# Hybrid block: intermediate stores on GpSimd's DMA queue, and two normed blocks turned from SBUF

## The chip, the cores and the metric

The kernel runs on one core of one Trainium2 chip. The metric is the device time of one execution, in microseconds (us). Engines are called as the profile calls them: PE (TensorE matmul), PEld (its weight load), DVE (VectorE), ACT (ScalarE), POOL (GpSimd) and SP (SyncE). SP computes nothing here; its queue issues most of the DMAs. A DMA issued by POOL stands in POOL's own instruction stream: POOL works its rows off in order, and a row that waits holds everything behind it. The same holds for SP.

## The reference

Two equal layers work on 1024 rows of 1024 fp32 numbers. Each is a mixer (four different heads, not touched here) and a feed-forward part, and both are wrapped in norms. What matters for this change is the end of the second layer:

```python
x = x + rms_norm(y @ w_out, g_post_mix)
h = rms_norm(x, g_pre_ffn)
x = x + rms_norm(conv_ffn(h, ...), g_post_ffn)

def conv_ffn(h, w_up, conv_w, conv_b, w_down):
    a, b = jnp.split(h @ w_up, 2, axis=-1)
    a = causal_dwconv(a, conv_w) + conv_b          # three taps along the rows
    return (jax.nn.gelu(a, approximate=True) * b) @ w_down
```

`w_up` has 2 x 2816 columns, that is 22 blocks `f` of 128 for `a` and as many for `b`.

## The kernel before, in words

All products are of fp32 accuracy: every operand is split into a high part (an ACT cast) and a low part (a DVE subtraction), and three matmuls give one product. The rows are worked in two halves of 512 (`h` 0 and 1), a half in four blocks `b` of 128.

**The last layer's feed-forward part** runs in these stages, in this order:

1. For half 0 the first six `f` are made early and plainly, in the midst of the mixer of half 1: `plain_up` (L1038) computes `c`, the gated result of one `f`, and stores it to a DRAM buffer `gD`.
2. `out(l, 1, y, True)` (L976) makes `y @ w_out` for the four blocks of half 1, and `norms` (L310) makes the two norms of each block. The normed blocks stand in four SBUF tiles, `oqf`, `okt`, `org` and `osu` (blocks 0 to 3). L324 also stores each to a DRAM buffer `hnD`; the blocks of half 0 were stored there earlier in the same way.
3. `plain_down` (L1048) multiplies the six early `f` of half 0 with `w_down` and stores the sums (`accD`).
4. `up_phase` takes new pools over the same SBUF, `rows` (L1088) names seven pairs of tiles (`A11`, `S1`, `S2`, `A12`, `S3`, `Q4`, `A22`, high and low), and `build` (L1095) fills them for one half. What follows is a fast matrix product of the Strassen-Winograd kind: seven products in place of eight, on sums of row blocks and column halves. `build` works on pairs of blocks. For each pair it loads two normed blocks from `hnD` (tiles `hn`), makes four sums on POOL (tiles `sa` and `sb`), turns the seven operands by 28 transposes on PE into seven PSUM banks, and puts each bank into its tile by an ACT cast (L1120) and a DVE subtraction (L1121). In the text that follows, one such cast with its subtraction is a "put".
5. `up_f` (L1133) makes one `f`: it loads the weight rows (`wraw`), makes seven weight operands `w` from them (ACT casts L1145, DVE subtractions L1146 and DVE sums L1150), runs the seven products (L1129 to L1131), and the gate (L1197 to L1202: ACT, two DVE, ACT with the gelu, two DVE), and stores `c` to `gD` (L1203). It runs first for `f` 0 and 1 of half 1 alone, right after `build(l, 1)`. Then comes `build(l, 0)`, and then all others: `f` 2 to 5 for half 1 alternate with `f` 6 to 21 for both halves.
6. `down_full` (L1205) loads `gD` and `w_down` again (tiles `graw` and `wraw`), splits both into tiles `g`, and adds all up; `end_block` makes the last norm.

**What sets the order.** A scheduler puts each engine's instructions into one fixed row when the program is built, by priorities in the code (`high_priority`) and by when tiles come free; on the chip each engine and each queue works its row off in order and waits by semaphores. Pools over the same SBUF are another source of waits: a tile of `up_phase` can only be written when the tile of the mixer that lay there has been read for the last time.

## Time and profile before

| what | us |
|---|---|
| median of 3 timed runs | 2526.83 (2521.61 to 2527.08) |
| profiled execution, its own time | 2522.4 |
| its span in the trace | 2520.6 |
| mean granted PE clock in it | 0.981 |
| PE busy | 2423.0 (96%) |
| DVE busy | 1777.1 (71%) |
| ACT busy | 971.6 (39%) |
| POOL busy | 251.7 (10%) |
| DMA, all queues | 281.33 MB, mean 112 GB/s |

Of the DMA bytes 266.37 MB go by the hardware queue that SP feeds and 12.65 MB by POOL's. In the trace a row has a start, a length, the engine, the source line, what it writes and reads, how many instructions it joins (x2), and, in brackets, the idle time of the engine ahead of it with what ended it. A row of SPq is the issue of a DMA, not the transfer.

### The profile page before, as it was taken

What the parts mean: (1) busy time and instruction counts of PE and PEld (TensorE: products, weight loads), DVE (VectorE), ACT (ScalarE), POOL (GpSimd) and SP (SyncE); (2) the same over time, 40 slices, a digit from 0 to 9 for tenths busy, and PEclk for the clock granted to TensorE, in tenths of its full rate; (3) what the DMA queues carried; (4) which work ended last, traced back from release to release, by engine and by line L of the source; (5) the groups of instructions that cost most, each with busy time, mean ns of one, the idle gap of its engine ahead of it and who ended that gap; (6) DMA issues with size and microseconds to landing.
All of it is one profiled execution on the core that took longest, in us unless ns stands there. A gap on an engine that the chain in (4) does not pass through costs nothing.

```text
span 2520.6 us, 36318 instructions
## 1 busy us (share of the span) xinstructions
PE 2423.0 (96%) x14020; PEld 2023.0 (80%) x14020; DVE 1777.1 (71%) x3659; ACT 971.6 (39%) x1510; POOL 251.7 (10%) x351
## 2 busy tenths in 40 slices
PE   8989998999999999899999999989888999998998
PEld 7968887877788987787778898877767888886887
DVE  8895699765655888955565589886567876664547
ACT  6333452423333453342332255233345444434212
POOL 2321103000000022200000001211003000000000
PEclk9999999999999999999999999999898999998999
DMA  5233343322233552222222355323363222215424
GB/s 185 72 90 111 126 135 92 103 80 76 80 100 109 161 166 84 76 94 77 84 84 85 124 167 188 92 82 110 117 226 118 101 92 83 77 59 201 141 67 151
DMA packets 100496, 281.33 MB, mean 112 GB/s; under 512 B 30482, under 2 KB 30802, under 8 KB 99812
## 3 DMA queue, kind: packets, MB, share of 16 engines
q1 hardware_dynamic: 96548, 266.37, 32.2%
q0 software_dynamic: 3776, 12.65, 1.5%
q8 instruction: 110, 1.80, 0.3%
q14 instruction: 62, 0.51, 0.1%
HBM read 239.11 MB, written 39.88 MB: 111 GB/s over the span
## 4 chain that ended last, share of the span: by engine, by line
PE 77%; DVE 14%; DMA 3%; issue 3%; ACT 2%; POOL 0%; SPq 0%; DVEq 0%; ACTq 0%; POOLq 0%
PE psg L213 9%; PE psg L214 9%; PE psg L212 9%; PE psg L1286 3%; PE psg L1288 3%; PE psg L1287 3%; DVE pr L839 3%; PE psg L233 3%; PE psg L1129 3%; PE psg L1131 3%; PE psg L1130 3%; PE psg L234 3%; PE psg L235 3%; DVE wlo L203 2%; DVE A L841 2%
## 5 line engine op out<-in xcount | busy, mean ns | idle before, releaser
L212 PE MATMUL psg<-hT,whi 128*128 128x512 f32 x1248 | 496.4, 398 | 0.6 <-DVE rs L286 0.5
L213 PE MATMUL psg<-hT,whi 128*128 128x512 f32 x1248 | 496.4, 398 | 0.0
L214 PE MATMUL psg<-hT,wlo 128*128 128x512 f32 x1248 | 494.9, 398 | 0.0
L202 ACT CAST whi<-raw 128x1024 fp32r<-128x1024 f32 (+1 forms) x272 | 283.4, 1049 | 530.7 <-PE psg L213 217.8
L203 DVE TENSOR_TENSOR wlo<-raw,whi 128x1024 fp32r<-128x1024 f32 (+1 forms) x249 | 307.4, 1240 | 142.2 <-ACT whi L202 138.1
L213 PEld LDWEIGHTS psg<-hT,whi 128*128 128x128 f32 x1248 | 234.9, 188 | 54.5 <-issue 0.9
L214 PEld LDWEIGHTS psg<-hT,wlo 128*128 128x128 f32 x1248 | 235.0, 188 | 54.0 <-issue 0.4
L212 PEld LDWEIGHTS psg<-hT,whi 128*128 128x128 f32 x1248 | 235.2, 188 | 53.4 <-issue 1.3
L1293 DVE TENSOR_TENSOR acc<-acc,psg 128x512 f32<-128x512 f32 x160 | 108.9, 685 | 74.7 <-PE psg L1288 74.2
L1145 ACT CAST w<-wraw 128x512 fp32r<-128x512 f32 x154 | 92.7, 619 | 176.5 <-PE psg L1131 109.9
L234 PE MATMUL psg<-wlo,hT 128*128 128x256 f32 (+1 forms) x512 | 148.7, 291 | 4.8 <-DVE wlo L203 4.3
L233 PE MATMUL psg<-whi,y 128*128 128x256 f32 x512 | 143.9, 286 | 6.5 <-DVE raw L1018 2.8
L233 PE MATMUL psg<-whi,hT 128*128 128x256 f32 (+1 forms) x512 | 146.4, 290 | 2.3 <-ACT tmp L434 1.1
L235 PE MATMUL psg<-whi,hT 128*128 128x256 f32 (+1 forms) x512 | 148.0, 290 | 0.0
L234 PE MATMUL psg<-wlo,y 128*128 128x256 f32 x512 | 144.0, 284 | 0.8 <-DVE rv L295 0.8
L235 PE MATMUL psg<-whi,y 128*128 128x256 f32 x512 | 142.7, 283 | 0.0
L1286 PE MATMUL psg<-whi,g 128*128 128x512 f32 x352 | 141.5, 404 | 0.0
L1146 DVE TENSOR_TENSOR w<-wraw,w 128x512 fp32r<-128x512 f32 x154 | 105.0, 696 | 51.1 <-ACT w L1145 50.6
L1287 PE MATMUL psg<-wlo,g 128*128 128x512 f32 x352 | 138.8, 394 | 0.0
L1288 PE MATMUL psg<-whi,g 128*128 128x512 f32 x352 | 138.6, 394 | 0.0
L839 DVE SCALAR_TENSOR_TENSOR pr<-A 64x1 f32<-64x1 f32 (+30 forms) x124 | 110.4, 890 | 8.6 <-POOL A L835 6.4
L234 PEld LDWEIGHTS psg<-wlo,hT 128*128 128x128 f32 x512 | 98.4, 192 | 8.5 <-DVE wlo L203 5.1
(488 smaller groups left out, 5151.4 us busy)
## 6 DMA issues: line engine op xcount, KB each, us to landing
raw<-in_wU SPq DMA_DIRECT2D x100, 512.0 KB, 3.5
raw<-in_wA SPq DMA_DIRECT2D x56, 512.0 KB, 3.5
raw<-in_wD SPq DMA_DIRECT2D x50, 512.0 KB, 3.6
wraw<-in_wU SPq DMA_DIRECT2D x22, 1024.0 KB, 4.9
raw<-in_wO SPq DMA_DIRECT2D x40, 512.0 KB, 3.7
raw<-in_wB SPq DMA_DIRECT2D x24, 512.0 KB, 3.6
xs<-xb SPq DMA_DIRECT2D x24, 512.0 KB, 3.5
graw<-gD SPq DMA_DIRECT2D x22, 512.0 KB, 4.5
```

The costliest lines, as they stand in the source:

```text
L202: nc.scalar.copy(hi[:, :n], raw[:, :n])
L203: eng.tensor_tensor(lo[:, :n], raw[:, :n], hi[:, :n].bitcast(F32), ALU.subtract)
L212: nc.tensor.matmul(ps, a[0], b[0], start=first, stop=False)
L213: nc.tensor.matmul(ps, a[0], b[1], start=False, stop=False)
L214: nc.tensor.matmul(ps, a[1], b[0], start=False, stop=last)
L233: self.nc.tensor.matmul(ps[:, :width], h0, hi[:, s], start=k == 0, stop=False)
L234: self.nc.tensor.matmul(ps[:, :width], h0, lo[:, s], start=False, stop=False)
L235: self.nc.tensor.matmul(ps[:, :width], h1, hi[:, s], start=False, stop=k == len(hT) - 1)
L839: V.scalar_tensor_tensor(pr[:, 0:i, 0:i], A[:, 0:i, 0:i], -1.0, A[:, 0:i, i].unsqueeze(1).to_broadcast([64, i, i]), ALU.mult, ALU.mult)
L1286: nc.tensor.matmul(ps, hi[:, tb], us[i][0][:, s], start=i == 0, stop=False)
L1287: nc.tensor.matmul(ps, hi[:, tb], us[i][1][:, s], start=False, stop=False)
L1288: nc.tensor.matmul(ps, lo[:, tb], us[i][0][:, s], start=False, stop=i == len(g0) - 1)
```

## The change

Three things are changed in the last layer's feed-forward part.

- Stores go from SP's queue to POOL's: the normed blocks to `hnD` (L324), and `c` to `gD` in `plain_up` (L1046) and in `up_f` (L1203). The loads of `hn` in `build` (L1104) go to POOL's queue as well.
- Blocks 2 and 3 of half 1 are no longer stored to `hnD`. A new `build_early`, called after `plain_down`, makes the four sums from `org` and `osu` in SBUF and turns the seven operands into seven PSUM banks. After `up_phase` and `rows`, `build(l, 1)` handles only the pair of blocks 0 and 1, and `put` then empties the seven banks.
- The order of the seven operands in `build` becomes A11, S1, S2, A12, S3, Q4, A22.

```diff
@@ norms
-                if keep is not None:
-                    nc.sync.dma_start(keep[b * P:b * P + P], hn[b])
+                if keep is not None and not (keep_early and b > 1):
+                    nc.gpsimd.dma_start(keep[b * P:b * P + P], hn[b])
@@ out
-                self.norms(raw, hn, gpost, gpre, src, dst, keep, blocks)
+                self.norms(raw, hn, gpost, gpre, src, dst, keep, blocks, True)
@@ plain_up
-            self.nc.sync.dma_start(self.gD[l][f, :, h * HALF:h * HALF + HALF], c)
+            self.nc.gpsimd.dma_start(self.gD[l][f, :, h * HALF:h * HALF + HALF], c)
@@ build
+    def sums(self, xs, bufs):
+        L, R = slice(0, 512), slice(512, 1024)
+        s1, s2, q4, s3 = bufs
+        G = self.nc.gpsimd
+        G.tensor_tensor(s1, xs[1][:, L], xs[1][:, R], ALU.subtract)
+        G.tensor_tensor(s2, s1, xs[0][:, L], ALU.subtract)
+        G.tensor_tensor(q4, s2, xs[0][:, R], ALU.add)
+        G.tensor_tensor(s3, xs[0][:, L], xs[1][:, L], ALU.subtract)
+        return (("A11", xs[0][:, L]), ("S1", s1), ("S2", s2), ("A12", xs[0][:, R]), ("S3", s3), ("Q4", q4),
+                ("A22", xs[1][:, R]))
+
+    def turned(self, p, x):
+        for k in range(4):
+            self.nc.tensor.transpose(p[:, k * P:k * P + P], x[:, k * P:k * P + P], self.ident)
+        return p.rearrange("p (k t) -> p k t", k=4)
+
+    def put(self, n, p4, h, i):
+        cs = slice(h * 256 + i * P, h * 256 + i * P + P)
+        hi, lo = self.A[n]
+        self.nc.scalar.copy(hi[:, :, cs], p4)
+        self.nc.vector.tensor_tensor(lo[:, :, cs], p4, hi[:, :, cs].bitcast(F32), ALU.subtract)
+
+    def build(self, l, h, pairs=(0, 1)):
         nc = self.nc
-        for i in range(2):
+        for i in pairs:
             xs = []
             for e in range(2):
                 x = self.cbuf("hn")
                 r0 = h * HALF + (2 * i + e) * P
-                nc.sync.dma_start(x[:, :D], self.hnD[l][r0:r0 + P])
+                nc.gpsimd.dma_start(x[:, :D], self.hnD[l][r0:r0 + P])
                 xs.append(x)
             sa, sb = self.cbuf("sa"), self.cbuf("sb")
...
+            for j, (n, x) in enumerate(self.sums(xs, (sa[:, 0:512], sa[:, 512:1024], sb[:, 0:512], sb[:, 512:1024]))):
+                self.put(n, self.turned((self.ps, self.pq)[j % 2](), x), h, i)
+
+    def build_early(self, hn):
+        banks = (self.ps, self.pq, lambda: self.pq("h"))
+        return [(n, self.turned(banks[j % 3](), x)) for j, (n, x) in
+                enumerate(self.sums([hn[2], hn[3]], [self.tmp() for _ in range(4)]))]
@@ up_f
-        nc.sync.dma_start(self.gD[l][f, :, halves[0] * HALF:halves[0] * HALF + 2 * N], c)
+        nc.gpsimd.dma_start(self.gD[l][f, :, halves[0] * HALF:halves[0] * HALF + 2 * N], c)
@@ run
-        self.out(l, 1, y, True)
+        hn = self.out(l, 1, y, True)
         self.plain_down(l)
+        late = self.build_early(hn)
         self.up_phase()
         self.rows(l)
-        self.build(l, 1)
+        self.build(l, 1, (0,))
+        for n, p4 in late:
+            self.put(n, p4, 1, 1)
         self.up_f(l, 0, (1,), 0)
```

The change makes the file 12 lines longer from `build` on, so that L1104 becomes L1124, L1120 becomes L1114, and L1203 becomes L1215.

How the instructions stand in the engines' rows is shown at three places. The first is ACT behind the last copy of `plain_down` (`acc`), where the first `build` and the weights of `f` 0 are made. Before, the weight casts of `f` 0 (`w_17726` and on) came first:

```order
L1078 COPY acc_17534<-psg_17555 128x512
L1145 CAST w_17726<-wraw_17724 128x512
L1145 CAST w_17730<-wraw_17724 128x512
L1145 CAST w_17733<-wraw_17724 128x512
L1145 CAST w_17738<-wraw_17724 128x512
L1145 CAST w_17741<-wraw_17724 128x512
L1145 CAST w_17744<-wraw_17724 128x512
L1120 CAST A11h_17592<-psg_17616 128x4x128
L1145 CAST w_17748<-wraw_17724 128x512
```

Now the seven casts from the early banks come first:

```order
L1078 COPY acc_17532<-psg_17553 128x512
L1114 CAST A11h_17633<-psg_17582 128x4x128
L1114 CAST S1h_17635<-psm_17587 128x4x128
L1114 CAST S2h_17637<-psh_17592 128x4x128
L1114 CAST A12h_17639<-psg_17597 128x4x128
L1114 CAST S3h_17641<-psm_17602 128x4x128
L1114 CAST Q4h_17643<-psh_17607 128x4x128
L1114 CAST A22h_17645<-psg_17612 128x4x128
L1157 CAST w_17722<-wraw_17720 128x512
L1157 CAST w_17726<-wraw_17720 128x512
L1157 CAST w_17729<-wraw_17720 128x512
L1157 CAST w_17734<-wraw_17720 128x512
```

The weights of `f` 0 moved behind seven puts; DVE's row has the same order. The tile `A11h` lies where a mixer tile that the sixth early bank is turned from lay, so the first of these casts waits for that bank's transposes.

The second place is the second build, `build(l, 0)`. Before, its loads stood on SP, between the stores of `f` 0 (`c_17758`) and `f` 1 (`c_17891`), and POOL held only its sums:

```order
L1203 DMA gD1_109<-c_17758 128x512
L1104 DMA hn_17990<-hnD1_107 128x1024
L1104 DMA hn_17992<-hnD1_107 128x1024
L1140 DMA wraw_18374<-in_wU 128x2x1024
L1104 DMA hn_18049<-hnD1_107 128x1024
L1203 DMA gD1_109<-c_17891 128x512
L1104 DMA hn_18051<-hnD1_107 128x1024
```

Now POOL's row holds the stores, the loads and the sums:

```order
L1215 DMA gD1_109<-c_17754 128x512
L1124 DMA hn_17986<-hnD1_107 128x1024
L1124 DMA hn_17988<-hnD1_107 128x1024
L1215 DMA gD1_109<-c_17887 128x512
L1099 TENSOR_TENSOR sa_17990<-hn_17988 128x512
L1102 TENSOR_TENSOR sb_17991<-hn_17986,hn_17988 128x512
L1100 TENSOR_TENSOR sa_17990<-sa_17990,hn_17986 128x512
L1101 TENSOR_TENSOR sb_17991<-sa_17990,hn_17986 128x512
L1124 DMA hn_18045<-hnD1_107 128x1024
L1124 DMA hn_18047<-hnD1_107 128x1024
L1099 TENSOR_TENSOR sa_18049<-hn_18047 128x512
L1102 TENSOR_TENSOR sb_18050<-hn_18045,hn_18047 128x512
```

The first pair's sums moved behind the store of `f` 1 (`c_17887`), and both loads of the second pair moved behind those sums. On PE the transposes of the second pair are followed by twelve S1 products of `f` 2 and ten of the twelve of `f` 6, which stood ahead of its last transposes before; twelve A12 products of `f` 2 moved ahead of the whole build.

The third place is SP at the start of `down_full`. Its row is now:

```order
L1152 DMA wraw_20631<-in_wU 128x2x1024
L1229 DMA graw_20794<-gD1_109 128x1024
L1229 DMA graw_20803<-gD1_109 128x1024
L1229 DMA graw_20876<-gD1_109 128x1024
L1227 DMA wraw_20792<-in_wD 128x1024
L1227 DMA wraw_20801<-in_wD 128x1024
```

Before, the stores of the last `f` stood in this row too, three ahead of the first `graw` and one between the second and the third. The third `graw` still stands ahead of both `wraw`.

More of the change, by code (lines that the diff above doesn't have):

```diff
@@ L308, in sumsq, with norms @@
         return self.rstd(ss, 1, 1.0 / D)
-    def norms(self, raw, hn, gpost, gpre, src, dst, keep=None, blocks=range(NB)):
+    def norms(self, raw, hn, gpost, gpre, src, dst, keep=None, blocks=range(NB), keep_early=False):
         nc = self.nc
@@ L1093, in rows @@
             self.A[n] = (hi, lo)
-    def build(self, l, h):
+    def sums(self, xs, bufs):
[18 more added lines that the diff above has]
+    def build(self, l, h, pairs=(0, 1)):
         nc = self.nc
-        V, A = nc.vector, self.A
-        for i in range(2):
-            cs = slice(h * 256 + i * P, h * 256 + i * P + P)
+        for i in pairs:
             xs = []
@@ L1103, in build @@
                 r0 = h * HALF + (2 * i + e) * P
-                nc.sync.dma_start(x[:, :D], self.hnD[l][r0:r0 + P])
+                nc.gpsimd.dma_start(x[:, :D], self.hnD[l][r0:r0 + P])
                 xs.append(x)
-            L, R = slice(0, 512), slice(512, 1024)
             sa, sb = self.cbuf("sa"), self.cbuf("sb")
-            G = nc.gpsimd
-            G.tensor_tensor(sa[:, L], xs[1][:, L], xs[1][:, R], ALU.subtract)
-            G.tensor_tensor(sa[:, R], sa[:, L], xs[0][:, L], ALU.subtract)
-            G.tensor_tensor(sb[:, R], sa[:, R], xs[0][:, R], ALU.add)
-            G.tensor_tensor(sb[:, L], xs[0][:, L], xs[1][:, L], ALU.subtract)
-            for i_, (n, x, s) in enumerate((("A11", xs[0], L), ("A12", xs[0], R), ("A22", xs[1], R), ("S1", sa, L),
-                                            ("S2", sa, R), ("S3", sb, L), ("Q4", sb, R))):
-                p = (self.ps, self.pq)[i_ % 2]()
-                for k in range(4):
-                    nc.tensor.transpose(p[:, k * P:k * P + P], x[:, s][:, k * P:k * P + P], self.ident)
-                p4 = p.rearrange("p (k t) -> p k t", k=4)
-                hi, lo = self.A[n]
-                nc.scalar.copy(hi[:, :, cs], p4)
-                V.tensor_tensor(lo[:, :, cs], p4, hi[:, :, cs].bitcast(F32), ALU.subtract)
+            for j, (n, x) in enumerate(self.sums(xs, (sa[:, 0:512], sa[:, 512:1024], sb[:, 0:512], sb[:, 512:1024]))):
[4 more added lines that the diff above has]
+                enumerate(self.sums([hn[2], hn[3]], [self.tmp() for _ in range(4)]))]
     def product(self, ps, a, b, cs, first, last):
```

## Prediction

> **What bounds the kernel now.** I first read PE's busy time by stretches (columns: start and end, length, then busy us and instruction count of PE, PEld, DVE, ACT and POOL, granted clock, DMA share, GB/s), since PE is busy for 96% of the span and only a stretch in which it is idle can give time back.
>
> ```profile
> 1880.40:1888.00 7.60, 0.37 (x2) 0.40 (x3) 5.71 (x9) 3.87 (x7) 0.00 (x0) 0.77 0.81 287
> 1888.00:1900.00 12.00, 8.61 (x41) 6.94 (x39) 10.59 (x16) 6.62 (x13) 7.53 (x6) 0.64 0.46 176
> 1900.00:1922.70 22.70, 22.32 (x184) 22.12 (x184) 18.90 (x33) 12.22 (x25) 4.44 (x5) 0.97 0.13 49
> 1922.70:1943.70 21.00, 15.38 (x90) 13.39 (x91) 15.60 (x25) 11.18 (x20) 11.55 (x11) 0.84 0.48 174
> ...
> 1960.00:2280.00 320.00, 320.00 (x1507) 263.76 (x1506) 219.45 (x316) 134.80 (x212) 2.92 (x17) 1.00 0.23 81
> ```
>
> From 1960 to 2280, where the steady `up_f` run, PE has no gap at full clock: a store or load moved between queues there can give nothing. Around the two builds PE is idle for 19.6 - 8.98 = 10.6 us up to 1900 and for 5.6 us in the second build's stretch. These are the places that the change touches. Next I read PE's rows there, with what ended each wait.
>
> ```profile
> 1887.63 1.08 PE L1117 MATMUL psg<-ident,hn 128*128 128x128 f32 x4 [7.29 <-DMA hn<-hnD]
> ...
> 1922.72 0.39 PE L1129 MATMUL psg<-A22h,w 128*128 128x256 f32 x1 [0.40 <-DVE a L1193]
> 1926.52 0.63 PE L1117 MATMUL psg<-ident,hn 128*128 128x128 f32 x4 [2.15 <-DMA hn<-hnD]
> ...
> 1939.09 0.37 PE L1129 MATMUL psm<-S1h,w 128*128 128x256 f32 x1
> ...
> 1940.60 0.60 PE L1117 MATMUL psg<-ident,sa 128*128 128x128 f32 x4
> ...
> 1943.36 0.60 PE L1117 MATMUL psg<-ident,sb 128*128 128x128 f32 x4
> 1943.72 0.37 PE L1129 MATMUL psg<-A11h,w 128*128 128x256 f32 x1
> ```
>
> The first build begins with 7.29 us of waiting for normed rows from DRAM, the second with 2.15. My measuring point is 1943.72, where the A11 product of `f` 2 starts and PE is gapless from then on; what is early or late there is early or late at the end.
>
> **The first build: a gain, which DVE limits.** Removed are two loads of `hn` and one wait: the pair `org`, `osu` is turned from SBUF, and its sums are made before `plain_down` ends.
>
> ```profile
> 1867.28 1.28 DVE L322 SCALAR_TENSOR_TENSOR osu<-xb,rs,oap 128x1024 f32<-128x1024 f32 x1
> 1881.51 0.69 DVE L1146 TENSOR_TENSOR w<-wraw,w 128x512 fp32r<-128x512 f32 x1 [12.95 <-ACT w L1145]
> ...
> 1888.90 1.27 POOL L1109 TENSOR_TENSOR sa<-hn 128x512 f32<-128x512 f32 x1 [89.08 <-DMA hn<-hnD]
> ...
> 1880.40:1922.70 42.30, 35.20 (x56) 0.84 0.35 128
> ```
>
> `osu` is ready at 1868.56, POOL has been idle for 89 us, and four sums of 1.27 take 5.1 us: done at 1873.7, some 7 us before `plain_down` ends at 1880.4. They cost nothing; a delay of over 7 us would be needed to uncover them. The 28 early transposes take at least 7 x 0.36 = 2.5 us (four of them from 1943.36 to 1943.72) and fit into the wait of 7.29, which the other pair's loads still have: their first one waits for `plain_down`'s last matmul either way.
>
> But PE alone doesn't set the end of this stretch. The last row (DVE alone; busy, count, clock, DMA share, GB/s) shows DVE with 35.2 us of work in the 42.3 us up to `f` 1's last product, and that work stays: 14 puts, the weights, the gates. DVE is idle for 7.1 us, 1.1 of them before 1881.51. In the changed order DVE starts with the early puts, whose first cast waits for six turned banks, 6 x 0.36 = 2.2 us after 1880.4, and for its own ACT cast (some 0.6): DVE begins near 1883.2, that is 1.7 us later than now. If it then never waited, it would be done 6.0 - 1.7 = 4.3 us earlier, and some 6 if the operations that POOL now slows run at their usual length as well. If it waits as much as now, it is done about 1 us later. I take a **gain of 3 us** at the end of `f` 1, with ends of 6 and -1.
>
> **The second build: a loss.** Here the rows of SP, POOL, ACT and DVE are needed together.
>
> ```profile
> 1921.81 0.32 SPq L1203 DMA_DIRECT2D gD<-c  x1
> 1922.23 1.28 SPq L1104 DMA_DIRECT2D hn<-hnD  x2
> 1923.80 0.38 SPq L1140 DMA_DIRECT2D wraw<-in_wU  x1
> 1926.54 0.32 SPq L1104 DMA_DIRECT2D hn<-hnD  x1
> 1930.72 0.32 SPq L1203 DMA_DIRECT2D gD<-c  x1
> 1931.50 0.32 SPq L1104 DMA_DIRECT2D hn<-hnD  x1
> ...
> 1927.79 1.54 POOL L1109 TENSOR_TENSOR sa<-hn 128x512 f32<-128x512 f32 x1 [23.27 <-ACT A11h L1120]
> 1929.29 2.18 POOL L1112 TENSOR_TENSOR sb<-hn 128x512 f32<-128x512 f32 x1
> ...
> 1932.78 1.26 POOL L1111 TENSOR_TENSOR sb<-sa,hn 128x512 f32<-128x512 f32 x1
> 1935.16 1.28 POOL L1109 TENSOR_TENSOR sa<-hn 128x512 f32<-128x512 f32 x1 [1.12 <-DMA hn<-hnD]
> ...
> 1938.98 1.29 POOL L1111 TENSOR_TENSOR sb<-sa,hn 128x512 f32<-128x512 f32 x1
> ```
>
> ```profile
> 1927.67 0.59 ACT L1120 CAST A12h<-psm 128x512 fp32r<-128x512 f32 x1
> 1928.15 0.64 ACT L1200 ACTIVATE c<-c 128x512 f32<-128x512 f32 x1
> ...
> 1925.64 0.74 DVE L1199 SCALAR_TENSOR_TENSOR c<-a,pf,c 128x512 f32<-128x512 f32 x1
> ...
> 1930.25 0.41 DVE L1202 TENSOR_TENSOR c<-c,psg 128x256 f32<-128x256 f32 x1
> ```
>
> Now the second pair's first load goes out at 1926.54, its second one right behind the store of `f` 1, at 1931.50, and lands 3.66 us later, at 1935.16; sums until 1940.27. In the changed order POOL's row has both stores, all four loads and all sums, and the second pair's loads stand behind the first pair's sums, which stand behind the store of `f` 1. What one issue costs POOL, and how long POOL's loads take, is bounded by its other DMAs (the last three rows: KB each, median us from issue to landing):
>
> ```profile
> 2461.49 0.54 POOL L1253 DMA_DIRECT2D xb<-xs  x1 [183.80 <-DVE g L208]
> ...
> xs<-xb SPq DMA_DIRECT2D x24, 512.0 KB, 3.5
> ...
> hn<-hnD SPq DMA_DIRECT2D x8, 512.0 KB, 5.8
> xb<-xs POOLq DMA_DIRECT2D x8, 512.0 KB, 4.7
> ```
>
> The chain, with the gain of 3:
> - The gate of `f` 0 is done when its store goes out, at 1921.8 now and at 1918.8 then. Store and two loads at 0.54 each: the second load is out at 1920.4.
> - Landing: 3.7 (a lone load, above) to 5.8, the median of SP's `hn` loads. SP's pair here took 4.3 (1922.23 to 1926.52); POOL's median of 4.7 is near. I take 4.6: the first pair is there at 1925.0.
> - The gate of `f` 1 ends at 1930.66 now. Its gelu starts at 1928.15, behind two puts' casts, though its input was ready at 1926.38; in the changed order the gelu stands ahead of those casts. That gives up to 1.77, and with DVE's share I take 1.9: 1930.66 - 1.9 - 3 = 1925.8. The store's issue takes it to 1926.3, when POOL may begin the sums; the loads are there.
> - Four sums take 6.25 now (1927.79 to 1934.04, DVE busy beside them) or 5.11 (the second pair). I take 5.8: 1932.1.
> - Two issues: each 0.54. The second load goes out at 1932.6 and is there at 1937.2. DMA bandwidth isn't what holds it: it is issued late.
> - Second sums 5.11: 1942.35, against 1940.27 now. The last turn, 0.5: 1942.85.
> - PE's order: twelve S1 products of `f` 2 (1939.09 to 1940.60) and ten of `f` 6 (to 1943.36), 1.51 + 2.41 = 3.9 us, ran ahead of the last transposes and now run behind them. Twelve A12 products of `f` 2, as many and as wide as the first twelve, go ahead of the build instead: -1.5. So +2.4, and A11 of `f` 2 would stand where it does now at 1942.85 + 2.4 = 1945.3.
>
> That is **1.6 us later than 1943.72**. The first build's 3 us are given back, and 1.6 more. The sum's low end (gain 6, landing 3.7, sums 5.11) is 3.0 us earlier than now; its high end (gain -1, no earlier gelu, landing 5.8, sums 6.25) is 9 us later.
>
> **Moves that cost nothing or next to it.** In the steady stretch POOL is busy for 2.92 of 320 us; the stores' issues, 0.54 each, hide beside PE, and what they would delay are the small writes ahead of a later `f`. Ahead of the first build the moved stores stand in POOL's row before a few POOL operations of the mixer; one of them may start up to one norm operation later (1.28), which I put at 0, with an end of +1.
>
> **The start of `down_full`, where freeing SP seems to be worth most.** The longest wait of all stands there, and SP's stores are in the queue.
>
> ```profile
> 2303.40 0.80 PE L1235 MATMUL psm<-g 128*128 128x512 f32 x1 [12.57 <-ACT g L207]
> ...
> 2295.07 1.22 DVE L208 TENSOR_TENSOR g<-graw,g 128x1024 fp32r<-128x1024 f32 x1
> ...
> 2296.31 0.32 SPq L1217 DMA_DIRECT2D graw<-gD  x1
> 2296.68 8.28 SPq L1215 DMA_DIRECT2D wraw<-in_wD  x3
> ```
>
> The first weights (`wraw`) go out at 2296.68, behind the third `graw`, and that one waits for DVE's split of the first `graw`, which ends at 2296.29 and stands behind the last gate. With the stores gone the third `graw` is still ahead of `wraw` and still waits for that split. So nothing of the 12.57 is gained.
>
> **The sum.** -3 at the first build, +4.6 at the second, 0 elsewhere: +1.6, called **+2** with the end of +1 ahead of the builds counted in part. The profiled execution took 2522.4, of which 2520.6 are span; it would take 2524.4. It is 4.4 under the median of the timed runs, so against these the forecast is 2526.83 + 2 = **2528.8 us**. A measurement of this kernel can tell about 0.2%, some 5 us, from no change, so this counts as the same.
>
> **Rivals.**
> 1. *The first build gives all of its idle time* (faster). If the weights are not needed as early as DVE's row makes them, PE's 10 us are gained rather than 3, and the same chain gives 1.6 - 7 = -5.4: 2521.4. For it: PE's wait of 7.29 goes, and the clock was 0.64 while PE waited. Against it: DVE's 35.2 of 42.3.
> 2. *SP's row is freed for `down_full`* (faster). If the weights went out with the first `graw`, they would be there before the last gate's end, and PE would start about one split and one cast behind 2296.3, near 2298: 5 us earlier, so 2523. The order speaks against it.
> 3. *POOL's issues are held by DVE* (slower). The sum that took 2.18 instead of 1.28 beside a busy DVE shows that POOL is held at times. If each issue is held by that 0.9 (1.44 in place of 0.54) and the landing is 5.8, the first pair is there at 1918.8 + 4.3 + 5.8 = 1928.9, its sums (6.25) end at 1935.1, the second pair lands at 1942.4, its sums end at 1947.5, and A11 comes at 1950.4: +6.7, **2533.5**. It decides as soon as landing and issue together are some 3 us longer than I took. The Trainium skill, SBUF — State Buffer, section "SBUF: two separate sides", box on the "DVE blocks DMA" trap, says that a POOL-issued DMA's descriptors can't be written while DVE runs an operation in its two-port mode, and gives some 620 ns alone against 3100 overlapped. By that figure five held issues would be an estimated 12 us, and the time 2539. No row here shows such a DMA beside a busy DVE; DVE's operations in this stretch are nearly all of two inputs, which the page names as a conflict only with a POOL operation that reads SBUF.
>
> **Chances and range.** My forecast, within 5 us of no change, 0.47; rival 1 0.20 and rival 2 0.04, with small gains beyond them 0.01, so faster 0.25; rival 3 and what else makes it later 0.28. The likeliest case's own range is 2523.8 to 2536. The whole range starts at 2519, below rival 1, since the runs before spread by 5.5, and ends at 2537, between rival 3 and the sum's high end.
>
> **What would show it.** Right: PE turns the first pair at 1880.4 with hardly a wait; `f` 1's A22 ends some 3 us earlier; POOL issues the second pair near 1932; the second build's PE waits grow from 5.6 to about 10 us; the wait of 12.57 stays. Wrong: the second pair lands before 1935 (faster), POOL's issue rows last well over 0.54 (slower), or gaps appear between 1960 and 2280, where I left nothing for POOL to do harm.

## The result, and the profile after

| | before | after |
|---|---|---|
| median of the timed runs, us | 2526.53 (2521.61 to 2527.08) | 2539.31 (2536.06 to 2543.5) |
| profiled execution, its own time, us | 2522.4 | 2536.06 |
| its span, us | 2520.6 | 2534.2 |

The ratio after to before is **1.0058**, with an interval of 1.0042 to 1.0074: the change makes the kernel slower by some 15 us (11 to 19); by the medians it is 12.8. I had forecast 2528.8 with a range of 2519 to 2537 and called it no change. The time lies above the range and on another side of the bound.

To see where the time went I cut both traces at the same seven points of the program. All but the sixth are starts of an instruction: POOL's split `wlo` of a mixer weight of 128x1056 (near 1510 us), ACT's first `AT<-AT` of L734 (near 1554), POOL's load `ozf` (near 1800), `plain_down`'s last matmul (near 1880), the last A22 product of `f` 1, PE's idling ahead of `down_full`, and the end of that wait.

| stretch, us | before | after | difference |
|---|---|---|---|
| up to the split | 1510.06 | 1509.92 | -0.1 |
| split to first `AT` (mixer of half 1) | 44.02 | 45.77 | +1.8 |
| first `AT` to `ozf` | 245.19 | 244.42 | -0.8 |
| `ozf` to the end of `plain_down` | 80.67 | 83.30 | +2.6 |
| to the last A22 of `f` 1 (first build) | 44.16 | 44.34 | +0.2 |
| to the end of the up products (second build and the steady part) | 366.73 | 373.52 | +6.8 |
| wait at `down_full` | 12.57 | 15.18 | +2.6 |
| the rest | 217.20 | 217.75 | +0.6 |
| span | 2520.6 | 2534.2 | +13.6 |

The point near 1510 itself lay between 1507.1 and 1516.3 in the fourteen profiled kernels, ahead of all that was changed. Whole times therefore scatter by more than a single stage is worth, and for what one part of the change does I compare the stretches. A stretch that nothing touches scatters too: from the first `AT` to `ozf` it took 244.3 to 246.0, and both builds with the steady part took 409.3 to 411.0 in the three kernels that leave them as they were (the kernel before, `e8_weights_early` and `e9_norm_stores_only`).

**What came as forecast.** The view by stretches of the kernel after (columns as in the prediction), cut at the end of `plain_down`, the last A22 of `f` 1, and 1960:

```profile
1883.41:1927.75 44.34, 32.09 (x237) 30.35 (x236) 37.70 (x58) 24.08 (x46) 10.15 (x11) 0.81 0.31 109
1927.75:1960.00 32.25, 21.32 (x115) 18.48 (x114) 17.72 (x30) 12.71 (x23) 11.73 (x13) 0.79 0.29 105
1960.00:2280.00 320.00, 320.00 (x1524) 264.50 (x1523) 224.28 (x326) 137.41 (x218) 11.97 (x36) 1.00 0.23 83
```

PE is still gapless from 1960 to 2280, though POOL's row is now busier there (11.97 against 2.92 us): the moved stores do no harm in the steady part. But in the first build PE is idle for 44.34 - 32.09 = 12.3 us, where it was 44.16 - 33.08 = 11.1 before (the same stretch of the kernel before):

```profile
1879.94:1924.10 44.16, 33.08 (x237) 30.84 (x236) 36.22 (x58) 24.14 (x46) 11.98 (x10) 0.85 0.36 133
```

The early turn removed the wait of 7.29 and gained nothing. PE's waits of the kernel after, in the two builds, show what took its place:

```profile
1889.75 0.63 PE L1108 MATMUL psg<-ident,hn 128*128 128x128 f32 x4 [2.89 <-DVE A12l L1115]
1892.56 1.11 PE L1108 MATMUL psm<-ident,sa 128*128 128x128 f32 x4 [2.18 <-POOL sa L1099]
...
1903.25 1.11 PE L1108 MATMUL psg<-ident,hn 128*128 128x128 f32 x4 [5.37 <-DVE A11l L1115]
...
1930.42 0.63 PE L1108 MATMUL psg<-ident,hn 128*128 128x128 f32 x4 [2.39 <-DMA hn<-hnD]
1934.66 1.11 PE L1108 MATMUL psm<-ident,sa 128*128 128x128 f32 x4 [3.61 <-POOL sa L1099]
...
1944.96 1.12 PE L1108 MATMUL psm<-ident,sa 128*128 128x128 f32 x4 [1.98 <-POOL sa L1099]
```

Up to 1903 PE waits for DVE most of all; in the second build it waits for the loads and for POOL's sums, 10.9 us in all (5.6 before; some 10 forecast). The first three experiments separate the parts of the change, the others follow one stage each.

### The profile page after: what moved, and what is told of

The parts are those of the page before. It is cut to its first block, busy times and chain, and to the rows that moved or that the text cites. A ratio compares the mean times of both kernels' runs of the same rounds, so it can differ in the third digit from the quotient of the medians.

```text
span 2534.2 us, 36313 instructions
## 1 busy us (share of the span) xinstructions
PE 2420.1 (95%) x14020; PEld 2021.1 (80%) x14020; DVE 1779.9 (70%) x3659; ACT 971.8 (38%) x1510; POOL 273.2 (11%) x391
## 4 chain that ended last, share of the span: by engine, by line
PE 75%; DVE 15%; issue 4%; DMA 3%; ACT 2%; POOL 1%; SPq 0%; DVEq 0%; ACTq 0%; POOLq 0%
PE psg L213 9%; PE psg L214 9%; PE psg L212 9%; PE psg L1298 3%; DVE pr L839 3%; PE psg L1300 3%; PE psg L1299 3%; PE psg L233 3%; PE psg L234 3%; PE psg L235 3%; PE psg L1143 3%; PE psg L1141 3%; PE psg L1142 3%; DVE wlo L203 2%; DVE A L841 2%
```

## The experiments

Each is named by its label. Kernels of one group were timed on one chip against the same runs of the kernel before: the first four (before: 2523.27), the next four (2524.25), the last four (2523.72); the kernel after was timed against the runs of the first table. Three dots in a diff or a view stand for lines left out.

### Which part of the change: e1_queues_only, e2_early_only, e3_loads_on_sp

`e1_queues_only` is the kernel before with the stores of L324, L1046 and L1203 and the loads of L1104 on POOL's queue:

```diff
-                    nc.sync.dma_start(keep[b * P:b * P + P], hn[b])
+                    nc.gpsimd.dma_start(keep[b * P:b * P + P], hn[b])
...
-            self.nc.sync.dma_start(self.gD[l][f, :, h * HALF:h * HALF + HALF], c)
+            self.nc.gpsimd.dma_start(self.gD[l][f, :, h * HALF:h * HALF + HALF], c)
...
-                nc.sync.dma_start(x[:, :D], self.hnD[l][r0:r0 + P])
+                nc.gpsimd.dma_start(x[:, :D], self.hnD[l][r0:r0 + P])
...
-        nc.sync.dma_start(self.gD[l][f, :, halves[0] * HALF:halves[0] * HALF + 2 * N], c)
+        nc.gpsimd.dma_start(self.gD[l][f, :, halves[0] * HALF:halves[0] * HALF + 2 * N], c)
```

> The kernel before with every move to POOL's queue (stores of the normed blocks and of c, loads of hn), but without the early turn. Theory A (the loss comes from what stands behind what in POOL's row: second build +6.8, the load of gpost behind the last store +2.6, the stores beside the loads of w_down +3.5): nearly the whole loss, 12 to 15 us over the kernel before, with the second build's last loads issued some 6 us late and the wait at the start of down_full near 15 instead of 12.6. Rival B (the early turn and the puts ahead of the weights are to blame): at most 4 us over the kernel before.

`e2_early_only` is the kernel after with these four lines back on SP's queue (the diff the other way round), so it has the early turn and the new order of operands alone.

> The kernel after with all stores and loads back on SP's queue, so that the early turn stands alone. Theory A: 2 to 5 us faster than the kernel before, since the first build's gain stays and nothing is given back in the second. Rival B: slower than the kernel before by 3 us or more. If the weights behind the early puts run beside POOL's sums, DVE's L1158 and L1162 there take up to twice their usual 0.69, which would hold the gain of the first build near 0.

`e3_loads_on_sp` is the kernel after with only the loads back:

```diff
-                nc.gpsimd.dma_start(x[:, :D], self.hnD[l][r0:r0 + P])
+                nc.sync.dma_start(x[:, :D], self.hnD[l][r0:r0 + P])
```

> The kernel after with only the loads of hn back on SP. Theory A: the second pair's loads no longer stand behind the first pair's sums, so that the second build ends 4 to 7 us earlier than in the kernel after; total 5 to 9 us over the kernel before (the parts ahead of plain_down's end and at down_full stay). Rival C (the loads are late because POOL's queue lands them later, not because they are issued late): less than 2 us of change.

| | median | ratio to before (interval) | split to `AT` | `ozf` to `plain_down` | first build | second build and steady part | wait at `down_full` |
|---|---|---|---|---|---|---|---|
| before | 2523.27 | | 44.02 | 80.67 | 44.16 | 366.73 | 12.57 |
| after | 2539.31 | 1.0058 (1.0042 to 1.0074) | 45.77 | 83.30 | 44.34 | 373.52 | 15.18 |
| e1_queues_only | 2538.4 | 1.0063 (1.0048 to 1.0078) | 47.56 | 81.57 | 45.04 | 372.80 | 15.15 |
| e2_early_only | 2529.1 | 1.0017 (1.0006 to 1.0027) | 43.85 | 81.14 | 43.15 | 370.85 | 12.49 |
| e3_loads_on_sp | 2537.0 | 1.0053 (1.0038 to 1.0068) | 46.29 | 85.05 | 43.89 | 370.92 | 15.42 |

The queues alone cost as much as the whole change. The early turn with the new order of operands, where I had expected a gain of 2 to 5, costs some 4 us (1.5 to 6.8). The two don't add up: on top of the moved queues they cost the builds nothing more (first build, second build and steady part together take 417.8 in `e1_queues_only` and 417.9 in the kernel after). With the loads back on SP, 2.6 us of the 6.8 in the second build go (4 to 7 expected), and the time hardly moves. So the loads behind the sums, where I had put nearly all of the loss, are one part of several. Two others lie ahead of the builds, and one at `down_full`.

### Ahead of the builds: e9_norm_stores_only, e10_first_stores_on_sp

`e9_norm_stores_only` is the kernel before with only the norm's stores moved:

```diff
-                    nc.sync.dma_start(keep[b * P:b * P + P], hn[b])
+                    nc.gpsimd.dma_start(keep[b * P:b * P + P], hn[b])
```

> The kernel before with one thing changed: the stores of the normed blocks (eight, L324) go by POOL's queue. The rows of PE, DVE and ACT are the same. Theory G (these stores cost time twice, far ahead of the builds: POOL's small copies of the delta rule wait behind those of half 0, and those of half 1 travel beside the loads of w_down instead of behind or ahead of them in one queue): from POOL's 128x1056 split near 1510 to the first AT activation near 1554 it takes 46 to 47.5 us instead of 43.8; from the load of ozf near 1800 to plain_down's last matmul 82 to 84 instead of 80.7; total 4 to 6 us over the kernel before. Rival H (these stretches differ by chance from one execution to the next): both as before, total within 2 us.

`e10_first_stores_on_sp` is the kernel after with these stores and `plain_up`'s (L1046) back on SP's queue.

> The kernel after with the stores of the norms and of plain_up back on SP; those of up_f and all loads of hn stay on POOL. Theory G: the two stretches above fall back to 43.8 and 80.7, total 4 to 6 us under the kernel after. Rival H: no change beyond 2 us.

| | ratio to before (interval) | split to `AT` | `ozf` to `plain_down` |
|---|---|---|---|
| e9_norm_stores_only | 1.0013 (1.0003 to 1.0022) | 45.71 | 82.89 |
| e10_first_stores_on_sp | 1.0043 (1.0028 to 1.0058) | 43.10 | 79.94 |

One moved line brings both delays, and taking it back, together with `plain_up`'s store, removes both. Over all profiles, the first stretch took 43.1 to 44.5 in the six kernels that store the normed rows by SP and 45.7 to 48.3 in the eight that do so by POOL (means 43.7 and 46.9: **+3.2**); the other one 79.9 to 81.1 and 80.5 to 85.1 (means 80.5 and 82.9: **+2.4**; here the two groups touch). The two delays have different causes.

POOL's row in the mixer, of the kernel before and then of the kernel after (time line; in brackets the idle time before a row and what ended it):

```profile
1529.20 2.69 POOL L203 TENSOR_TENSOR wlo<-raw,whi 128x1024 fp32r<-128x1024 f32 x1 [16.41 <-ACT whi L202]
1531.84 0.34 POOL L463 COPY tmp<-cq 128x3 f32<-128x3 f32 x2
1546.95 4.25 POOL L463 COPY tmp<-cq 128x3 f32<-128x3 f32 x1 [14.78 <-DMA dd<-tmp]
```

```profile
1529.81 0.55 POOL L324 DMA_DIRECT2D hnD<-acc  x1 [12.09 <-DVE rs L282]
1530.38 2.42 POOL L203 TENSOR_TENSOR wlo<-raw,whi 128x1024 fp32r<-128x1024 f32 x1
1541.64 0.56 POOL L324 DMA_DIRECT2D hnD<-acc  x1 [8.84 <-DVE rt L283]
1542.20 1.59 POOL L463 COPY tmp<-cq 128x3 f32<-128x3 f32 x2
1546.67 5.15 POOL L463 COPY tmp<-cq 128x3 f32<-128x3 f32 x2 [2.88 <-DMA dd<-tmp]
```

Two tiny copies (128x3) that start a mixer head ran at 1531.84. Now a store stands ahead of them in POOL's row, and the store waits until DVE has normed its block, at 1541.64. The copies run 10 us later than before. That the delay runs through them is read from this order, and from `e10_first_stores_on_sp`, where they stand right behind the split again (1531.39 and 1534.04) and the delay is gone. In all eight kernels that store by POOL the copies are as late as here, in the six others as early as before; no run moved the copies alone.

The other delay lies where `oqf` and `okt` are stored while `w_down` is loaded for `plain_down`. DMA issues from 1795 to 1865, before and then after (KB each, median us from issue to landing):

```profile
raw<-in_wD SPq DMA_DIRECT2D x6, 512.0 KB, 4.4
...
```

```profile
raw<-in_wD SPq DMA_DIRECT2D x6, 512.0 KB, 5.3
...
hnD<-oqf POOLq DMA_DIRECT2D x1, 512.0 KB, 6.1
```

The stores used to wait in SP's row, one behind the other with the loads; on a queue of their own they move at the same time, and the median weight load takes 0.9 longer. In the six kernels that store by SP the median is 4.1 to 4.4, in seven of the eight others 4.9 to 5.4. The eighth is `e11_up_stores_on_sp`: there the loads took 4.1, and the stretch 80.5, as short as with the stores on SP. So the delay goes with the slower loads, and stores on the second queue don't slow them every time. The Trainium skill, DMA: Bandwidth & Descriptors, section "Queues, rings and completion order", says that each DMA engine takes packets in turn from every queue that has work for it; these rows agree with that. That the slower loads are what ends `plain_down` later is read from ACT's longest wait for `raw<-in_wD` near 1850, 3.86 before and 4.89 after; no run moved the loads alone.

### The first build: e12_no_sums

The early turn should have given 3 us. The first early put waits for the sixth turned bank, as forecast, and the weights of `f` 0 come behind the seven puts, beside POOL's sums of the other pair. DVE, and then POOL, of the kernel after:

```profile
1887.27 0.69 DVE L1115 TENSOR_TENSOR A11l<-psg,A11h 128x512 fp32r<-128x512 f32 x1 [15.14 <-ACT A11h L1114]
...
1891.47 1.58 DVE L1158 TENSOR_TENSOR w<-wraw,w 128x512 fp32r<-128x512 f32 x1
1893.09 3.32 DVE L1162 TENSOR_TENSOR wraw<-wraw 128x512 f32<-128x512 f32 x2
1896.33 2.36 DVE L1158 TENSOR_TENSOR w<-wraw,w 128x512 fp32r<-128x512 f32 x2
```

```profile
1891.24 1.26 POOL L1099 TENSOR_TENSOR sa<-hn 128x512 f32<-128x512 f32 x1 [5.91 <-DMA hn<-hnD]
1892.47 1.71 POOL L1102 TENSOR_TENSOR sb<-hn 128x512 f32<-128x512 f32 x1
1894.14 1.71 POOL L1100 TENSOR_TENSOR sa<-sa,hn 128x512 f32<-128x512 f32 x1
```

The five DVE operations take 7.26. Over the whole stretch DVE's loss and gain cancel: it began 3.9 behind `plain_down`'s last matmul instead of 1.6 (1881.51 before), which costs 2.3; its work grew from 36.22 to 37.70, which costs 1.5; and its idle time behind its start fell from 6.4 to 2.8, which gives 3.6. `e12_no_sums` leaves out the four sums of that pair: plain halves of the normed blocks are turned in place of S1, S2, S3 and Q4.

```diff
-            sa, sb = self.cbuf("sa"), self.cbuf("sb")
-            for j, (n, x) in enumerate(self.sums(xs, (sa[:, 0:512], sa[:, 512:1024], sb[:, 0:512], sb[:, 512:1024]))):
+            sa, sb = (self.cbuf("sa"), self.cbuf("sb")) if h == 0 else (None, None)
+            ops = self.sums(xs, (sa[:, 0:512], sa[:, 512:1024], sb[:, 0:512], sb[:, 512:1024])) if h == 0 else [
+                (n, xs[e][:, s:s + 512]) for n, e, s in (("A11", 0, 0), ("S1", 1, 0), ("S2", 1, 0), ("A12", 0, 512),
+                                                         ("S3", 0, 0), ("Q4", 0, 512), ("A22", 1, 512))]
+            for j, (n, x) in enumerate(ops):
```

> The kernel after without the four sums of the first build's loaded pair (blocks 0 and 1 of half 1): the blocks themselves are turned in their place, so four of the seven operands of that pair hold other numbers; the transposes, puts and products are as many as before. Theory I (the gain of the first build is eaten by DVE and POOL slowing each other, since the weights of f 0 now run beside those sums): the DVE operations of f 0's weights there take their usual 0.69 each instead of up to 1.7, and from plain_down's end to f 1's last A22 it takes 39 to 41 us instead of 44.3. Rival J (the stretch is bound by DVE's order and the put of the loaded pair, whoever works beside it): 43 us or more, with the DVE operations at their usual length.

The same DVE operations in it:

```profile
1898.01 0.68 DVE L1161 TENSOR_TENSOR w<-wraw,w 128x512 fp32r<-128x512 f32 x1
1898.72 1.42 DVE L1165 TENSOR_TENSOR wraw<-wraw 128x512 f32<-128x512 f32 x2
1900.10 1.29 DVE L1161 TENSOR_TENSOR w<-wraw,w 128x512 fp32r<-128x512 f32 x2
```

They take 3.39 without the sums beside them: the sums cost DVE 3.9 us there. By the point of the first table, the last A22 of `f` 1, the first build takes 37.73 instead of 44.34. But twelve A12 products of `f` 2 that run ahead of that point in the kernel after run behind it here; up to the last product ahead of the second build it takes 39.09 (39 to 41 expected), which is 5.3 less. The rest of the 5.3 is that the transposes no longer wait for sums, so the run, timed once, does not price the slowing by itself. Nor does the slowing belong to the early turn alone: DVE's pair of sums beside POOL's took 3.31 also in the kernel before with only the new order of operands (`e6_before_new_order`), and 3.44 and 3.31 in the two kernels with the early turn and the old order. What the run shows is that the slowing is there, and that with the early turn and without the other pair's sums the first build is 5.1 shorter than before, more than the 3 us of the forecast. What leaving out the sums would be worth without the early turn no run shows.

### The second build: e5_early_old_order, e6_before_new_order, e7_after_old_order, e11_up_stores_on_sp

Before, `plain_down`'s last matmul stood at 1879.94 and the last sum ended at 1940.27, 60.3 later. POOL's row after:

```profile
1925.31 0.57 POOL L1215 DMA_DIRECT2D gD<-c  x1 [26.58 <-DVE c L1214]
1925.88 1.07 POOL L1124 DMA_DIRECT2D hn<-hnD  x2
1932.77 0.55 POOL L1215 DMA_DIRECT2D gD<-c  x1 [5.82 <-issue]
1933.34 1.27 POOL L1099 TENSOR_TENSOR sa<-hn 128x512 f32<-128x512 f32 x1
...
1938.34 1.10 POOL L1124 DMA_DIRECT2D hn<-hnD  x2
1943.65 1.26 POOL L1099 TENSOR_TENSOR sa<-hn 128x512 f32<-128x512 f32 x1 [4.21 <-DMA hn<-hnD]
...
1947.45 1.27 POOL L1101 TENSOR_TENSOR sb<-sa,hn 128x512 f32<-128x512 f32 x1
```

It is the chain that the prediction describes: the store of `f` 0, two loads, the store of `f` 1, sums, two loads, sums. The last one ends at 1948.72, 65.3 behind `plain_down`, 5.0 later than before. Behind it PE's order adds the rest. Four kernels take this apart.

Two put the operands back into the order of the kernel before, `e5_early_old_order` on `e2_early_only` and `e7_after_old_order` on the kernel after:

```diff
-        return (("A11", xs[0][:, L]), ("S1", s1), ("S2", s2), ("A12", xs[0][:, R]), ("S3", s3), ("Q4", q4),
-                ("A22", xs[1][:, R]))
+        return (("A11", xs[0][:, L]), ("A12", xs[0][:, R]), ("A22", xs[1][:, R]), ("S1", s1), ("S2", s2), ("S3", s3),
+                ("Q4", q4))
```

> The early turn alone, all DMAs on SP's queue as in the run with the early turn only, but with the seven operands turned in the order of the kernel before (A11, A12, A22, S1, S2, S3, Q4). The row of PE then has S1 products of f 2 and f 6 ahead of the last transposes of the second build again. Theory E (the new order of the operands costs the 3.9 us of those 22 products, since they no longer cover the wait for POOL's last sums): from f 1's last A22 to the last product of the up phase it takes about 367 us as in the kernel before, instead of 370.9; total 2 to 4 us under the run with the early turn only, level with or 1 to 2 us under the kernel before. Rival F (the second build is late because its loads or sums are late): 370 us or more again.

> The kernel after with nothing taken back but the order of the seven operands. Theory E: the same stretch falls from 373.5 to between 370 and 371, total 2 to 4 us under the kernel after, 9 to 12 over the kernel before; what stays in the second build is POOL's row. Rival F: no change beyond 1 us.

`e6_before_new_order` gives the kernel before the new order alone:

```diff
-            for i_, (n, x, s) in enumerate((("A11", xs[0], L), ("A12", xs[0], R), ("A22", xs[1], R), ("S1", sa, L),
-                                            ("S2", sa, R), ("S3", sb, L), ("Q4", sb, R))):
+            for i_, (n, x, s) in enumerate((("A11", xs[0], L), ("S1", sa, L), ("S2", sa, R), ("A12", xs[0], R),
+                                            ("S3", sb, L), ("Q4", sb, R), ("A22", xs[1], R))):
```

> The kernel before with nothing changed but the order of the seven operands (A11, S1, S2, A12, S3, Q4, A22). Theory E: from f 1's last A22 to the last product of the up phase 370 to 371 us instead of 366.7; total 3 to 5 us over the kernel before. Rival F: no change beyond 1 us.

`e11_up_stores_on_sp` is the kernel after with the store of `up_f` back on SP's queue:

```diff
-        nc.gpsimd.dma_start(self.gD[l][f, :, halves[0] * HALF:halves[0] * HALF + 2 * N], c)
+        nc.sync.dma_start(self.gD[l][f, :, halves[0] * HALF:halves[0] * HALF + 2 * N], c)
```

> The kernel after with only the stores of up_f back on SP. The rows of the other engines are nearly the same; POOL's row has no store between the first pair's loads and its sums, and the load of gpost no longer stands behind the last store. Theory A: the wait at the start of down_full falls from 15.2 to 12.6; the second build's first sums start 1 to 3 us earlier, and since the second pair's loads still stand behind the sums and the S1 products behind the last transposes, from plain_down's end to the last product of the up phase it takes 415 to 417 us (before 411, after 418); total 3 to 5 us under the kernel after. Rival (the store of f 1 costs nothing there): that stretch stays at 418.

In this table the first build ends with the last product ahead of the second build's transposes. That is the last A22 of `f` 1 as in the first table, but not where the early turn meets the old order: there the twelve A12 products of `f` 2 stand behind it. PE in `e5_early_old_order`:

```profile
1923.84 0.28 PE L1143 MATMUL psg<-A22h,w 128*128 128x256 f32 x1
1924.29 0.39 PE L1141 MATMUL psh<-A12h,w 128*128 128x256 f32 x1 [0.18 <-ACT w L1157]
...
1926.24 0.28 PE L1143 MATMUL psh<-A12h,w 128*128 128x256 f32 x1
```

| | ratio to before (interval) | first build | second build and steady part | both |
|---|---|---|---|---|
| before | | 44.16 | 366.73 | 410.9 |
| after | 1.0058 (1.0042 to 1.0074) | 44.34 | 373.52 | 417.9 |
| e1_queues_only | 1.0063 (1.0048 to 1.0078) | 45.04 | 372.80 | 417.8 |
| e2_early_only | 1.0017 (1.0006 to 1.0027) | 43.15 | 370.85 | 414.0 |
| e5_early_old_order | 1.0008 (0.9999 to 1.0018) | 43.79 | 369.30 | 413.1 |
| e6_before_new_order | 1.0011 (1.0000 to 1.0022) | 45.96 | 367.57 | 413.5 |
| e7_after_old_order | 1.0061 (1.0046 to 1.0076) | 43.13 | 371.98 | 415.1 |
| e3_loads_on_sp | 1.0053 (1.0038 to 1.0068) | 43.89 | 370.92 | 414.8 |
| e11_up_stores_on_sp | 1.0054 (1.0036 to 1.0071) | 45.05 | 372.39 | 417.4 |

Over both builds the new order costs 2.6 on the kernel before, 2.8 on the kernel after and 0.9 between `e2_early_only` and `e5_early_old_order`. In the second build and the steady part it costs 0.8, 1.5 and 1.6, less than half of the 3.9 that I had expected there; in the first build 1.8, 1.2 and -0.6. In that order the sums' transposes come second and third, ahead of two that need no sum. The early turn by itself shortens the first build by 0.4 (`e5_early_old_order` against the kernel before), 1.9 (`e7_after_old_order` against `e1_queues_only`) or 2.8 (`e2_early_only` against `e6_before_new_order`); over both builds, in the same order, it costs 2.2, gains 2.7 and costs 0.5. These are stage lengths of one profile each, and the smallest of these differences are no larger than the scatter. In the timed runs the new order alone on the kernel before is at the edge of what can be told, and on the kernel after the old order brought nothing that shows.

In `e5_early_old_order` the first build is no longer than before, and the second takes 2.6 more. Its rows (ACT, DVE, SP's queue) show how:

```profile
1930.48 0.59 ACT L1114 CAST A12h<-psm 128x512 fp32r<-128x512 f32 x1 [0.27 <-PE psm L1108]
1930.97 0.63 ACT L1212 ACTIVATE c<-c 128x512 f32<-128x512 f32 x1
...
1932.51 1.75 DVE L1162 TENSOR_TENSOR wraw<-wraw 128x512 f32<-128x512 f32 x1
1934.18 0.41 DVE L1214 TENSOR_TENSOR c<-c,psg 128x256 f32<-128x256 f32 x1
...
1934.66 0.32 SPq L1215 DMA_DIRECT2D gD<-c  x1
1935.09 0.37 SPq L1124 DMA_DIRECT2D hn<-hnD  x1
```

The gelu of `f` 1 stands behind two casts that need the first pair's load, its gate ends behind a DVE operation that a sum slows to 1.75, and the last load of the second pair waits behind its store in SP's row, until 1935.09. That is 52.6 behind `plain_down`, where it was 51.6 before (1931.50), although the store of `f` 0 went out 2.2 earlier. So an earlier `f` 0 doesn't bring the second build forward by itself: its last load hangs on the gate of `f` 1. In `e12_no_sums`, where both gates come over 5 us earlier than in the kernel after, the gain stays: both builds take 412.2, 5.7 less.

The store of `f` 1 ahead of the sums, which I had feared in POOL's row, costs nearly nothing: with it back on SP (`e11_up_stores_on_sp`) both builds together take 417.4 instead of 417.9.

### The wait at `down_full`: e4_gpost_late

The prediction said that the 12.57 would stay. It became 15.18. POOL, SP's queue, ACT and PE after:

```profile
2306.11 0.53 POOL L1215 DMA_DIRECT2D gD<-c  x1 [12.85 <-ACT g L207]
2306.64 0.53 POOL L301 DMA_DIRECT2D gpost<-in_gB  x1
...
2307.12 10.89 SPq L1227 DMA_DIRECT2D wraw<-in_wD  x3
...
2315.35 1.04 ACT L207 CAST g<-wraw 128x1024 fp32r<-128x1024 f32 x1 [10.15 <-DMA wraw<-in_wD]
...
2316.45 0.80 PE L1247 MATMUL psm<-g 128*128 128x512 f32 x1 [15.18 <-ACT g L207]
```

`gpost` is a load of 512 KB for the last norm, needed only at the very end. Before, POOL had nothing ahead of it:

```profile
2277.13 0.56 POOL L301 DMA_DIRECT2D gpost<-in_gB  x1 [38.05 <-PE psg L1131]
```

Now the last store of `c` stands ahead of it, waits for the last gate, and lets it go 0.5 us ahead of the weights that `down_full` is waiting for. `e4_gpost_late` moves this load to SP's queue, behind the first weights:

```diff
-        gpost = self.bcast(t["gB"][4 * l + 3], "gpost", pool=lambda n: self.py.tile([P, D], F32, tag="gpost", name=n, bufs=1))
...
+            if fs is groups[2]:
+                gpost = self.bcast(t["gB"][4 * l + 3], "gpost", eng=nc.sync, pool=lambda n: self.py.tile([P, D], F32, tag="gpost", name=n, bufs=1))
```

> The kernel after with the load of gpost (512 KB) taken out of POOL's row and issued by SP behind the first two weights of down_full. Theory A: the wait at the start of down_full falls from 15.2 back to 12.6, and the total by 2 to 3 us against the kernel after. Rival D (the wait grew because the last store itself lands later from POOL's queue): the wait stays at 15.

The wait is 12.96 in it. In `e11_up_stores_on_sp`, where the store is gone from POOL's row, `gpost` goes out early again and the wait is 12.04:

```profile
2298.19 0.56 POOL L301 DMA_DIRECT2D gpost<-in_gB  x1 [49.25 <-PE psm L1143]
2312.73 0.80 PE L1247 MATMUL psm<-g 128*128 128x512 f32 x1 [12.04 <-ACT g L207]
```

In the six kernels where `gpost` stands behind that store the wait is 15.2 to 15.7, in all others but the next one 11.6 to 13.0. The timed ratio of `e4_gpost_late`, 1.0056 (1.0037 to 1.0075), can't show 2 to 3 us; the stage does.

### The weights that come late: e8_weights_early

The wait of 12.57 had been read as weights that stand behind the third `graw`, and that behind the last gate, because of where their tiles lie. `e8_weights_early` is the kernel before with the pools of the down phase laid out in another order, so that `wraw` lies on tiles that are free earlier; nothing else is changed.

```diff
-        self.phase(("pa", 8), ("py", 12), ("pw", 2), ("pr", 2), ("pg", 6))
+        self.phase(("pw", 2), ("pr", 2), ("pa", 8), ("py", 12), ("pg", 6))
```

> Not a part of the change: the kernel before with the pools of down_full in another order in SBUF (pw and pr first), so that the first two weights and g rows of down_full no longer lie on tiles that the last gate uses and are loaded while the last products run. If the wait of 12.57 hangs on the late weights, it falls to 5 to 7 us (the last gate and the first splits are left), total 5 to 8 us under the kernel before. If it hangs on the splits behind the gate alone, nothing changes.

PE's first product of `down_full` and SP's queue in it:

```profile
2297.23 0.79 PE L1235 MATMUL psm<-g 128*128 128x512 f32 x1 [4.93 <-ACT g L207]
...
2283.66 0.42 SPq L1215 DMA_DIRECT2D wraw<-in_wD  x1
2284.18 0.74 SPq L1217 DMA_DIRECT2D graw<-gD  x1
```

The weights go out 8.6 us ahead of the wait's start at 2292.30 (2297.23 - 4.93), and the wait falls to 4.93. It takes 2516.53 us, a ratio of **0.9971** (0.9962 to 0.9981) to the kernel before: faster than both kernels of this study. The queue of the stores had no part in it.

## Why the prediction was wrong

The steps are those of the prediction.

- **"A gain of 3 us" in the first build: wrong.** It measured -0.2 (44.16 to 44.34). The wait of 7.29 went and the sums of the early pair cost nothing, as said; DVE was the limit, as said: it idled for 2.8 us behind its start. Two terms were mis-sized. DVE's late start was taken as 1.7 and measured 2.3. And its work, "that work stays", with "some 6 if the operations that POOL now slows run at their usual length", was to stay or to shrink: it grew by 1.5, because the overlap of DVE and POOL didn't shrink but moved. The weights of `f` 0 now run beside the other pair's sums, and five operations take 7.26 instead of 3.39. The 3.6 of waits that DVE did save went into these two. I had also given the order of the operands no price in the first build; in three pairs of kernels it measured 1.8, 1.2 and -0.6. How the loss divides between the order and the overlap stays open.
- **The chain of the second build: right up to the last sum.** Without the 3 us of gain it gives 1942.35 + 3 = 1945.35 for the end of the sums, 65.4 behind `plain_down`'s last matmul at 1879.94; measured 65.3. Most sizes were near what I took: issues of 0.53 to 0.57 (0.54), the gate of `f` 1 done 1.9 earlier with its gelu ahead of the puts (1.9), the second pair there 4.8 behind the start of its second issue at 1938.9 (4.6). But the first four sums took 5.0 and not 5.8, and the store of `f` 1 went out 0.5 behind its gate, for which I had no term: that the end fits to 0.1 is in part luck.
- **"-1.5" for twelve A12 products: a misreading.** These twelve products stood ahead of the build in the kernel before too (from 1920.8 on); nothing moved. I had it wrong in the account of PE's order as well. "The last turn, 0.5" was short also: PE's next product started 1.7 behind the last sum. And the start of A11 was a poor measuring point, since ten S1 products of `f` 6 that I had put ahead of it ran behind it. By the end of the up products, which is free of that, the two builds cost 7.0, where the prediction had 1.6. With the missing 3 of gain, the 1.5 of credit and the 1.2 of turn this makes 7.3.
- **"Moves that cost nothing or next to it": wrong by about 5 us.** The steady part cost nothing, as said. For the moved stores ahead of the builds I took 0 with an end of +1, from one norm operation of delay. The store that stands ahead of the copies waits for a whole block of the other half, and the copies came 10 us late (+3.2 in the means); and the stores beside the loads of `w_down` had no term at all (+2.4).
- **"Nothing of the 12.57 is gained": right, and not the whole of it.** I had asked what leaves SP's row there, and not what the same stores hold up in POOL's. `gpost` came late and cost 2.6.
- **The rivals.** Rival 1, PE's 10 us, did not occur. Rival 2, an earlier `wraw`, did not either, for the reason given; `e8_weights_early` shows that the weights were indeed worth about as much as I had put there (7.6 of wait against 5), and that other tiles bring it, which the freer queue of the kernel after did not. Rival 3 had the sign and the nearest time (2533.5), but not the reason: POOL's issues were not held. The store of `f` 0 and two loads went out while DVE ran without a gap from 1923.4 to 1933.4, operations of two SBUF inputs among them, such as this one of the kernel after:

```profile
1925.29 0.68 DVE L1158 TENSOR_TENSOR w<-wraw,w 128x512 fp32r<-128x512 f32 x1
```

  The issues beside them took 0.57 and, two together, 1.07 (1925.31 and 1925.88 above). The Trainium skill, SBUF — State Buffer, section "SBUF: two separate sides", names such a DVE operation as a conflict with a POOL operation that reads SBUF, which agrees with the sums and weights above, and the lock-out of descriptors for DVE's two-port mode, which no run here shows. The 2539 that the prediction worked out from that page's figure is the measured time by coincidence only.

Of the 13.6 us between the two profiles, 7.0 lie in the builds and the steady part, 4.4 in the two stretches with the norm's stores, 2.6 at `down_full`, and the remaining -0.4 in stretches that nothing touched (-0.1, -0.8 and +0.6). What is not settled: how much of the 3.2 and the 2.4, which are means over single profiles, is scatter, and why the head's 10 us of late copies come out as only 3.

## What to carry to other kernels

A DMA that is moved to a compute engine's queue brings its wait along: go through everything that stands behind it in that engine's row, the small copies and the loads for a much later stage too, and price the data that each store waits for, not its issue. Two transfers that used to follow each other in one queue can run side by side in two, and the one on the path can get slower. Before counting a gain in one stage, find the chain on which the next stage hangs: if the operation that starts it doesn't come earlier, the gain ends there. And when two kernels are compared up to a point, see that the same work lies ahead of it in both.

## What was not expected of the hardware

Elementwise sums on POOL and on DVE, both of two fp32 inputs in SBUF, slow each other by quite different factors: DVE's pair of L1162 took 3.32 instead of 1.42 us, while POOL's sums beside it took 1.71 instead of 1.27. With the stores of 512 KB on a second queue, the landing of loads of the same size took 5.3 us instead of 4.4 (4.9 to 5.4 in seven of eight kernels, 4.1 in one), though the DMA engines' busy share from 1795 to 1865 was 0.60 before and 0.56 after.
